# Down projection of an encoder layer: where the pieces of the second half's weights are kept, and in which order they are loaded

## The chip, the cores and the metric

The kernel runs on one core of a Trainium2 chip. The metric is the time of one execution on the device, in microseconds (us); lower is better. The profile names the engines PE (TensorE, matrix products; PEld is its weight load), DVE (VectorE), ACT (ScalarE), POOL (GpSimd) and SP (SyncE, which here only issues DMA transfers).

## The reference

One encoder layer over 1024 tokens of width 1024: a token mixer, a cross-attention and a gated feed-forward part, each followed by a layer norm. The change lies in the last product of the feed-forward part, `y @ w_down`, with `D_FF` = 2816 and `D` = 1024:

```python
def conv_ffn(x, w_up, b_up, w_dw, b_dw, w_down, b_down):
    h = x @ w_up + b_up
    h = lax.conv_general_dilated(h, w_dw[:, None, :], ...) + b_dw
    g, u = jnp.split(h, 2, axis=-1)
    y = jax.nn.gelu(g, approximate=False) * u
    return y @ w_down + b_down
...
    h = layer_norm(DN_ALPHA * h + conv_ffn(h, ...), ln3_w[l], ln3_b[l])
```

## The kernel before

**The product and its tiles.** The down projection contracts 22 slices of 128 features (`NFF` = 22, index `f`) for 8 tiles of 128 tokens (`NT` = 8, index `tt`) into 1024 columns, which are made in two halves of 512 (`c` = 0 and 1). Every operand is kept as a pair of 16-bit tiles, a high and a low part, and `mm3` makes each product with three matmuls of 128x512 (lines 225 to 227: high by high, high by low, low by high).

**Where y is kept.** `y` (22 slices) is written to DRAM by the stage before and comes back in pairs of slices: `y_pair(f, s)` loads a raw f32 tile named `ur` (a ring of two) and `split16` (lines 204 and 205) makes the pair: ACT writes the high part, DVE the low part. The pairs live in the tiles `yp` (list `yhome`, four slices to a tile); the sixth, `yhome[5]`, holds slices 20 and 21 in its first half and has two places free behind them. Slices 20 and 21 have a scale of their own, which a small matmul (`mx`) and five short DVE instructions work out shortly before (`y_scale(1)`, lines 184 to 177 and the one that writes `ratio`).

**Where the weights are kept.** `w_pair(j, c)` brings slices 4j to 4j+3 of half `c` (two slices for j = 5): one or two raw tiles `wraw` (a ring of two), each split by ACT and DVE into `whi` and `wlo`, which are rings of five. With six values of j and two halves the ring goes round more than twice, so a new piece waits until PE has done with the piece five places earlier. Only piece (5, 1), the last of half 1, has a place outside of the ring: the third slot of `yhome[5]`.

**The order of the work.** Half 0 is made first: for j = 0 to 4 a pass over the eight token tiles, which sum up in eight PSUM banks; a pass (the "NG loop", `NG` = 20) over slices 20 and 21 for the eight tiles follows, and DVE adds it to the copy `half0` with line 1773. Then the final loop takes one token tile after the other: 6 matmuls on slices 20 and 21 (bank `p2`), 60 matmuls on slices 0 to 19 (bank `p1`), the residual `r` (POOL lines 1792 and 1793, DVE line 1795), and the layer norm, whose result is written out. The residual rows of odd token tiles use the `wraw` ring too.

**What sets the order on each engine.** The program is written as above, with the calls of `w_pair` and `y_pair` between the token tiles, and a scheduler then places the instructions on each engine; every engine, and SP's DMA queue, works through its own list in order. Piece (5, 1) is the last `w_pair` of the program, and it is the first of half 1 that PE uses.

Of the kernel before, what the change touches and what calls it, by code (L numbers as in the profile page):

```python
# [8 lines left out]
F32 = mybir.dt.float32  # L9
# [47 lines left out]
def encoder(ctx, tc, I, out):  # L57
# [4 lines left out]
    def bcast_row(ap, n, off=0):  # L62
        return bass.AP(tensor=ap.tensor, offset=ap.offset + off, ap=[[0, 128], [1, n]])
# [15 lines left out]
    def bank(name):  # L79
        key = "mem" if name == "tk" else name  # L80
        turn[key] = turn.get(key, -1) + 1
        tag = SET[name][turn[key] % len(SET[name])]
        return pp.tile([128, 512], F32, name=name, tag=tag, bufs=NB[tag])
# [29 lines left out]
    def vec(i, name):  # L113
        t = vecs.tile([128, D], F32, name=f"vec{i}", tag=f"vec{i}")
        S.dma_start(t, bcast_row(I[name], D))
        return t
# [50 lines left out]
    def col(n=1):  # L167
        used[0] += n
        assert used[0] <= 96
        return sc[:, used[0] - n:used[0]]  # L170
# [32 lines left out]
    def split16(hi, lo, src, s):  # L203
        A.activation(hi, src, AF.Copy, scale=s)  # L204
        return V.scalar_tensor_tensor(lo, src, s, hi, op0=OP.mult, op1=OP.subtract)  # L205
# [76 lines left out]
    with ExitStack() as ca:  # L282

        yml = None
        with ExitStack() as cm:
# [254 lines left out]
            with ExitStack() as c2:  # L540
# [257 lines left out]
                with ExitStack() as c1:  # L798
# [7 lines left out]
                    for c in range(4):  # L806
                        w, ic = cw[2 + c]
                        for tt in range(NT):
# [6 lines left out]
                            j = slice(c % 2 * 256, c % 2 * 256 + 256)  # L815
# [407 lines left out]
    with ExitStack() as cb_:  # L1223
# [3 lines left out]
        f16 = lambda t: t.bitcast(F16)  # L1227
# [132 lines left out]
        def load_r(n):  # L1360
            if n < NT:
                rs[n] = rt.tile([128, D], F32, name="r", tag="r", bufs=5)
                S.dma_start(rs[n], h1_d[todo[n] * 128:todo[n] * 128 + 128, :])
# [74 lines left out]
        ur = cb_.enter_context(tc.tile_pool(name="unitraw", bufs=1, reuse_waits="tile"))  # L1438
# [126 lines left out]
        with ExitStack() as cE:  # L1565
# [69 lines left out]
            def y_pair(f, s):  # L1635

                raw = ur.tile([128, 2048], F32, name="ur", tag="ur", bufs=2)
                S.dma_start(raw.rearrange("p (f t) -> p f t", f=2), y_d[f:f + 2].rearrange("f p t -> p f t"))
                if f % 4 == 0:
                    tag = ("Yl", "X2h", "X1l", "X1h", "Yh", "X2l")[f // 4]  # L1640
                    pool = yp if tag[0] == "Y" else xp
                    yhome[f // 4] = f16(pool.tile([128, 4096], F32, name="yp", tag=tag)).rearrange(
                        "p (f n t) -> p f n t", f=4, n=2)
                for i in range(2):
                    t = yhome[f // 4][:, f % 4 + i]
                    split16(t[:, 0], t[:, 1], raw[:, i * SEQ:i * SEQ + SEQ], s)
                    ys[f + i] = t[:, 0], t[:, 1]

            def w_pair(j, c):

                n = min(4, NFF - 4 * j)
                if j == 5 and c == 1:
                    h, l = yhome[5][:, 2, 0], yhome[5][:, 2, 1]
                else:
                    h, l = (wp.tile([128, 2048], F16, name=t, tag=t, bufs=5) for t in ("whi", "wlo"))
                for i in range(n // 2):
                    raw = wp.tile([128, WP], F32, name="wraw", tag="wraw", bufs=2)[:, :1024]
                    S.dma_start(raw.rearrange("p (i c) -> p i c", i=2),
                                I["w_down"][2 * j + i].rearrange("p (i c) -> p i c", i=2)[:, :, c * 512:c * 512 + 512])
                    split16(h[:, i * 1024:i * 1024 + 1024], l[:, i * 1024:i * 1024 + 1024], raw, sd)  # L1660
                wdn[c, j] = tuple(t[:, :n * 512].rearrange("p (f c) -> p f c", c=512) for t in (h, l))

            def dmm(ps, tt, c, fs, first, last):
                t0 = slice(tt * 128, tt * 128 + 128)
                for f in fs:
                    wh, wl = wdn[c, f // 4]
                    mm3(ps, ys[f][0][:, t0], ys[f][1][:, t0], wh[:, f % 4, :], wl[:, f % 4, :],
                        first and f == fs[0], last and f == fs[-1])
# [3 lines left out]
            def y_scale(g):  # L1672
                sy[g] = scale_of(ysum[:, :NG] if g == 0 else ysum[:, NG:], 14)

            loaded = None
            for v in range(NFF):
# [25 lines left out]
                if v == NFF - 1:  # L1702
                    w_pair(0, 0)
# [20 lines left out]
            for tt in range(5):  # L1724
                ps[tt] = bank("dn")
                dmm(ps[tt], tt, 0, range(4), True, False)
                if tt == 0:
                    w_pair(1, 0)
                if tt in (1, 3):
                    y_pair(4 + tt - 1, s1)  # L1730
# [8 lines left out]
        with ExitStack() as cF:  # L1739
            wk = cF.enter_context(tc.tile_pool(name="wkF", bufs=1, reuse_waits="tile"))  # L1740
            inv = col(3)
            V.tensor_tensor(inv[:, 0:1], sd, s1, OP.mult)
            V.tensor_scalar(inv[:, 1:2], inv[:, 0:1], ALPHA, None, op0=OP.mult)
            V.tensor_scalar(inv[:, 2:3], inv[:, 0:1], inv[:, 0:1], EPS, op0=OP.mult, op1=OP.mult)
            al, ep = inv[:, 1:2], inv[:, 2:3]
            half0 = wk.tile([128, NT, 512], F32, name="half0")

            rw, rb, bd = vec(0, "ln2_w"), vec(1, "ln2_b"), vec(2, "b_down")
            V.tensor_scalar(rw, rw, al, None, op0=OP.mult)
            V.tensor_scalar(bd, bd, inv[:, 0:1], None, op0=OP.mult)  # L1750
            V.scalar_tensor_tensor(rb, rb, al, bd, op0=OP.mult, op1=OP.add)
            lw = vec(2, "ln3_w")
            for j in range(1, 5):
                for tt in range(NT):
                    dmm(ps[tt], tt, 0, range(4 * j, 4 * j + 4), False, j == 4)
                    if j == 4:
                        V.tensor_copy(half0[:, tt], ps[tt])
                    if tt in (0, 4) and j < 4:
                        y_pair(4 * j + 4 + tt // 2, s1)
                    if tt == 2:  # L1760
                        w_pair(j + 1, 0)
                    if j == 2 and tt == 6:
                        y_scale(1)
                        ratio = col()
                        V.tensor_scalar(ratio, sy[1][0], s1, 2.0 ** -14, op0=OP.mult, op1=OP.mult)
                    if j == 4 and tt == 0:
                        y_pair(NG, sy[1][1])
                    if j == 4 and tt in (4, 6):
                        w_pair((tt - 4) // 2, 1)
            for tt in range(NT):  # L1770
                p2 = bank("dn")
                dmm(p2, tt, 0, range(NG, NFF), True, True)
                V.scalar_tensor_tensor(half0[:, tt], p2, ratio, half0[:, tt], op0=OP.mult, op1=OP.add)
                if tt in (1, 3, 5):
                    w_pair(2 + tt // 2, 1)
            w_pair(5, 1)
            lb = yhome[5][:, 3].rearrange("p n t -> p (n t)").bitcast(F32)
            S.dma_start(lb, bcast_row(I["ln3_b"], D))
            rs = {}

            def load_r(tt):
                if tt < NT:
                    rs[tt] = (wp.tile([128, WP], F32, name="wraw", tag="wraw", bufs=2)[:, :D] if tt % 2 else
                              wk.tile([128, D], F32, name="r", tag="r", bufs=2))
                    S.dma_start(rs[tt], h2_d[tt * 128:(tt + 1) * 128, :])

            load_r(0)
            load_r(1)
            for tt in range(NT):
                load_r(tt + 2)  # L1790
                r = rs.pop(tt)
                G.tensor_tensor(r, r, rw, OP.mult)
                G.tensor_tensor(r, r, rb, OP.add)
                r0, r1 = r[:, :512], r[:, 512:]
                V.tensor_tensor(r0, r0, half0[:, tt], OP.add)
                p1, p2 = bank("dn"), bank("dn")
                dmm(p2, tt, 1, range(NG, NFF), True, True)
                V.scalar_tensor_tensor(r1, p2, ratio, r1, op0=OP.mult, op1=OP.add)
                dmm(p1, tt, 1, range(NG), True, True)
                V.tensor_tensor(r1, r1, p1, OP.add)  # L1800
                last = tt == NT - 1
                ln_tile(r, lw, lb, small, late=last, eps=ep, parts=2 if last else 1)
                for i in range(2 if last else 1):
                    c = slice(i * 512, i * 512 + 512) if last else slice(0, D)
                    (A if i else S).dma_start(out[tt * 128:(tt + 1) * 128, c], r[:, c])
# [87 lines left out]
```

## Time and profile before

| | us |
|---|---|
| median of 3 runs (lowest, highest) | 1573.36 (1570.8, 1579.4) |
| the profiled execution | 1571.99 |
| its span, first to last instruction | 1570.3 |

The profile is of one execution. The span is 1.7 us shorter than that execution's own time, which is what lies around it. The mean TensorE clock that was granted over the span is 0.976 of full speed (2.4 GHz).

### The profile page before, as it was taken

The page shows a single profiled execution, that of the slowest core. Times are in us where ns is not written, and L with a number is a line of the kernel's source. Part 1 is how long each engine was busy: PE and PEld are TensorE (multiplying, and loading weights), DVE is VectorE, ACT ScalarE, POOL GpSimd, SP SyncE. Part 2 cuts the span into 40 slices and gives each one's busy share as a digit, 9 for nine tenths or more (in the row PEclk, how much of TensorE's full clock was granted, in tenths as well). Part 3 has the DMA queues.
Part 4 walks back from the last instruction along what each step waited for, and adds up shares of the span by engine and source line. Part 5 has one row for each costly group of instructions (what it writes and reads, how often), then busy time and mean ns, then how long its engine had stood idle before and what let it go on. Part 6 is the DMA issues. An engine that isn't in the chain of part 4 may idle for free.

```text
span 1570.3 us, 21752 instructions
## 1 busy us (share of the span) xinstructions
PE 1476.7 (94%) x8134; PEld 881.3 (56%) x8134; DVE 1053.8 (67%) x1961; ACT 807.4 (51%) x1367; POOL 574.6 (37%) x446
## 2 busy tenths in 40 slices
PE   8798889999999899899999889999999999997998
PEld 6697767456766788774455434444444444443443
DVE  7984985445767777675457678788878878925333
ACT  5524544565554467523335668777777756611000
POOL 6423662412232766234112174444434420301342
PEclk9799999999999899999999989999999999998999
DMA  8743545323554743544001332222232434832111
GB/s 297 276 179 112 189 140 190 105 75 101 147 149 130 243 132 102 205 167 180 28 27 54 121 137 108 107 107 108 107 121 107 162 107 144 294 124 69 40 68 54
DMA packets 84896, 208.62 MB, mean 133 GB/s; under 512 B 7091, under 2 KB 36019, under 8 KB 81462
## 3 DMA queue, kind: packets, MB, share of 16 engines
q1 hardware_dynamic: 84496, 206.46, 37.9%
q8 instruction: 64, 1.05, 0.3%
q0 software_dynamic: 144, 0.49, 0.2%
q14 instruction: 42, 0.34, 0.1%
q10 hardware_dynamic: 150, 0.27, 0.0%
HBM read 158.34 MB, written 49.35 MB: 132 GB/s over the span
## 4 chain that ended last, share of the span: by engine, by line
PE 55%; DVE 20%; DMA 9%; ACT 9%; issue 4%; POOL 2%; SPq 1%; DVEq 0%; ACTq 0%; POOLq 0%
PE dn L227 5%; PE dn L226 5%; PE dn L225 5%; DMA sv<-in_w_down_dram 3%; PE S L225 3%; PE S L227 3%; PE S L226 3%; DVE wlo L205 3%; DVE cbuf L1586 2%; DVE cbuf L1587 2%; PE tk L225 2%; PE z L226 2%; PE z L227 2%; PE tk L226 2%; PE tk L227 2%
## 5 line engine op out<-in xcount | busy, mean ns | idle before, releaser
L225 PE MATMUL dn<-whi,yp 128*128 128x512 f16 x336 | 127.6, 383 | 1.4 <-ACT whi L204 1.4
L226 PE MATMUL dn<-wlo,yp 128*128 128x512 f16 x336 | 128.2, 382 | 0.0
L227 PE MATMUL dn<-whi,yp 128*128 128x512 f16 x336 | 128.2, 382 | 0.0
L1504 POOL TENSOR_TENSOR wraw<-ur 128x512 f32<-128x512 f32 x22 | 45.5, 2069 | 201.8 <-issue 187.3
L1586 DVE SCALAR_TENSOR_TENSOR cbuf<-C,wdw,cbuf 128x1024 f32<-128x1024 f32 x44 | 75.7, 1721 | 28.6 <-ACT cbuf L1585 28.5
L225 PEld LDWEIGHTS <-whi 128*128 128x128 f16 x540 | 53.6, 99 | 66.1 <-issue 7.7
L227 PEld LDWEIGHTS <-wlo 128*128 128x128 f16 x540 | 53.4, 99 | 59.8 <-DVE wlo L205 4.2
L226 PEld LDWEIGHTS <-whi 128*128 128x128 f16 x540 | 53.7, 99 | 54.6 <-issue 1.6
L205 DVE SCALAR_TENSOR_TENSOR wlo<-wraw,us,whi 128x1024 f16<-128x1024 f32 (+1 forms) x48 | 67.0, 1413 | 18.8 <-ACT whi L204 18.5
L253 ACT ACTIVATE r<-r,lnrs 128x1024 f32<-128x1024 f32 x19 | 23.6, 1243 | 101.7 <-DVE lnrs L252 101.7
L1587 DVE SCALAR_TENSOR_TENSOR cbuf<-C,wdw,cbuf 128x1024 f32<-128x1024 f32 x44 | 70.5, 1602 | 1.2
L204 ACT ACTIVATE whi<-wraw,us 128x1024 f16<-128x1024 f32 (+1 forms) x48 | 51.4, 1103 | 27.2 <-DVE us L177 22.3
L225 PEld LDWEIGHTS <-yp 128*128 128x128 f16 x352 | 34.6, 98 | 52.1 <-issue 11.5
L1585 ACT ACTIVATE cbuf<-C,bdw,wdw 128x1024 f32<-128x1024 f32 x44 | 54.5, 1238 | 10.5 <-DVE C L1622 9.7
L243 POOL TENSOR_TENSOR lnrs<-lnrs,mhalf 128x1 f32<-128x1 f32 x32 | 18.8, 589 | 110.7 <-DVE lnrs L242 93.1
L227 PEld LDWEIGHTS <-yp 128*128 128x128 f16 x352 | 34.6, 98 | 42.4 <-issue 1.4
L226 PEld LDWEIGHTS <-yp 128*128 128x128 f16 x352 | 34.7, 99 | 42.2 <-issue 1.4
L225 PE MATMUL tk<-whi,Bo 128*128 128x256 f16 (+1 forms) x192 | 53.6, 279 | 3.1 <-DVE stage L205 3.1
L226 PE MATMUL tk<-wlo,Be 128*128 128x256 f16 (+1 forms) x192 | 53.6, 279 | 2.1 <-DVE wlo L205 2.1
L225 PE MATMUL tk<-whi,Be 128*128 128x256 f16 (+1 forms) x192 | 53.9, 282 | 0.3 <-ACT whi L204 0.3
L227 PE MATMUL tk<-whi,Be 128*128 128x256 f16 (+1 forms) x192 | 53.6, 279 | 0.0
L226 PE MATMUL tk<-wlo,Bo 128*128 128x256 f16 (+1 forms) x192 | 53.2, 277 | 0.0
(496 smaller groups left out, 4855.4 us busy)
## 6 DMA issues: line engine op xcount, KB each, us to landing
ur<-in_w_up_dram SPq DMA_DIRECT2D x22, 1024.0 KB
sv<-in_w_down_dram SPq DMA_DIRECT2D x22, 512.0 KB
y<-cbuf SPq DMA_DIRECT2D x22, 512.0 KB
ur<-y SPq DMA_DIRECT2D x11, 1024.0 KB
wraw<-in_w_down_dram SPq DMA_DIRECT2D x22, 512.0 KB
r<-h SPq DMA_DIRECT2D x19, 512.0 KB
h<-r SPq DMA_DIRECT2D x16, 512.0 KB
wraw<-in_w_tok_dram SPq DMA_DIRECT2D x10, 512.0 KB
```

Source lines behind the costliest of these rows:

```text
L204: A.activation(hi, src, AF.Copy, scale=s)
L205: return V.scalar_tensor_tensor(lo, src, s, hi, op0=OP.mult, op1=OP.subtract)
L225: T.matmul(ps, lh, rh, start=first, stop=False, skip_group_check=skip)
L226: T.matmul(ps, lh, rl, start=False, stop=False, skip_group_check=skip)
L227: return T.matmul(ps, ll, rh, start=False, stop=last, skip_group_check=skip)
L243: G.tensor_tensor(rs[:, 0:1], rs[:, 0:1], mhalf[:, 0:1], OP.pow)
L253: A.activation(r, r, AF.Identity, scale=rs[:, 0:1], bias=rs[:, 1:2])
L1504: G.tensor_tensor(S1, A21, A22, OP.add)
L1585: A.activation(c, C[:, 1:SEQ + 1], AF.Identity, scale=wdw[:, 1, j:j + 1], bias=bdw[:, j:j + 1])
L1586: V.scalar_tensor_tensor(c, C[:, 0:SEQ], wdw[:, 0, j:j + 1], c, op0=OP.mult, op1=OP.add)
L1587: V.scalar_tensor_tensor(c, C[:, 2:SEQ + 2], wdw[:, 2, j:j + 1], c, op0=OP.mult, op1=OP.add)
```

## The change

Pieces (3, 1) and (4, 1) no longer go round the ring of five: each takes a tile of the `ur` ring, where the raw tiles of y were (one holds `h` in its first half and `l` in its second). Piece (5, 1) keeps its place but is now the first of half 1 to be loaded, even before (5, 0), and all the calls move up: token tiles 1, 3, 5, 7 of pass j = 4 call (5, 1), (0, 1), (1, 1), (2, 1), and token tiles 0 and 2 of the NG loop call (3, 1) and (4, 1).

```diff
@@ w_pair
                 if j == 5 and c == 1:
                     h, l = yhome[5][:, 2, 0], yhome[5][:, 2, 1]
+                elif j > 2 and c == 1:
+                    t = f16(ur.tile([128, 2048], F32, name="ur", tag="ur", bufs=2))
+                    h, l = t[:, :2048], t[:, 2048:]
                 else:
                     h, l = (wp.tile([128, 2048], F16, name=t, tag=t, bufs=5) for t in ("whi", "wlo"))
...
                     if j == 4 and tt == 0:
                         y_pair(NG, sy[1][1])
-                    if j == 4 and tt in (4, 6):
-                        w_pair((tt - 4) // 2, 1)
+                    if j == 4 and tt in (1, 3, 5, 7):
+                        w_pair((5, 0, 1, 2)[tt // 2], 1)
             for tt in range(NT):
                 p2 = bank("dn")
                 dmm(p2, tt, 0, range(NG, NFF), True, True)
                 V.scalar_tensor_tensor(half0[:, tt], p2, ratio, half0[:, tt], op0=OP.mult, op1=OP.add)
-                if tt in (1, 3, 5):
-                    w_pair(2 + tt // 2, 1)
-            w_pair(5, 1)
+                if tt in (0, 2):
+                    w_pair(3 + tt // 2, 1)
```

The instructions are the same in number on each engine; what moves is their order and the tiles that they name. Lines behind the first edit are three numbers higher after the change, those behind the last one two (1773 becomes 1776, 1795 becomes 1797).

ACT's list before the change, the splits of half 1's weights up to the final loop. The tiles `whi_12751`, `whi_12787`, `whi_12826`, `whi_12852`, `whi_12878` are pieces (0, 1) to (4, 1), and `yp_12688` is `yhome[5]`: its row with `ur_12686` is y's slices 20 and 21, its row with `wraw_12904` is piece (5, 1).

```order
L204 ACTIVATE whi_12751<-wraw_12753,sc_95 128x1024
L204 ACTIVATE whi_12751<-wraw_12757,sc_95 128x1024
L204 ACTIVATE whi_12787<-wraw_12789,sc_95 128x1024
L204 ACTIVATE whi_12787<-wraw_12793,sc_95 128x1024
L204 ACTIVATE whi_12826<-wraw_12828,sc_95 128x1024
L204 ACTIVATE whi_12826<-wraw_12832,sc_95 128x1024
L204 ACTIVATE yp_12688<-ur_12686,sc_95 128x1024 x2
L204 ACTIVATE whi_12852<-wraw_12854,sc_95 128x1024
L204 ACTIVATE whi_12852<-wraw_12858,sc_95 128x1024
L204 ACTIVATE whi_12878<-wraw_12880,sc_95 128x1024
L204 ACTIVATE whi_12878<-wraw_12884,sc_95 128x1024
L204 ACTIVATE yp_12688<-wraw_12904,sc_95 128x1024
```

ACT's list after the change, the same place; `whi_12723` is piece (5, 0), `whi_12742`, `whi_12778`, `whi_12814` are (0, 1) to (2, 1), `ur_12832` is (3, 1) and `ur_12857` (4, 1).

```order
L204 ACTIVATE yp_12688<-wraw_12706,sc_95 128x1024
L204 ACTIVATE whi_12723<-wraw_12725,sc_95 128x1024
L204 ACTIVATE whi_12742<-wraw_12744,sc_95 128x1024
L204 ACTIVATE whi_12742<-wraw_12748,sc_95 128x1024
L204 ACTIVATE whi_12778<-wraw_12780,sc_95 128x1024
L204 ACTIVATE whi_12778<-wraw_12784,sc_95 128x1024
L204 ACTIVATE whi_12814<-wraw_12816,sc_95 128x1024
L204 ACTIVATE whi_12814<-wraw_12820,sc_95 128x1024
L204 ACTIVATE ur_12832<-wraw_12833,sc_95 128x1024
L204 ACTIVATE ur_12832<-wraw_12837,sc_95 128x1024
L204 ACTIVATE yp_12688<-ur_12686,sc_95 128x1024 x2
L204 ACTIVATE ur_12857<-wraw_12858,sc_95 128x1024
```

Piece (5, 1) has moved from the last row to the first, ahead of (5, 0); y's slices 20 and 21 now stand behind both rows of (3, 1).

PE's list before the change, from the last matmul of the NG loop (`dn_12896`) into the final loop's first token tile (`dn_12919` is its bank `p2`, `dn_12918` its `p1`).

```order
L227 MATMUL dn_12896<-whi_12719,yp_12688 128x512
L225 LDWEIGHTS yp_12688
L225 MATMUL dn_12919<-yp_12688 128x512
L225 LDWEIGHTS yp_12043
L225 MATMUL dn_12918<-whi_12751,yp_12043 128x512
L226 LDWEIGHTS yp_12043
L226 MATMUL dn_12918<-wlo_12752,yp_12043 128x512
```

PE's list after the change, the same place (`dn_12917` is `p2`, `dn_12916` is `p1`).

```order
L227 MATMUL dn_12898<-whi_12723,yp_12688 128x512
L225 LDWEIGHTS yp_12688
L225 MATMUL dn_12917<-yp_12688 128x512
L226 LDWEIGHTS yp_12688
L226 MATMUL dn_12917<-yp_12688 128x512
L227 LDWEIGHTS yp_12688
L227 MATMUL dn_12917<-yp_12688 128x512
L225 LDWEIGHTS yp_12688
L225 MATMUL dn_12917<-yp_12688 128x512
L226 LDWEIGHTS yp_12688
L226 MATMUL dn_12917<-yp_12688 128x512
L227 LDWEIGHTS yp_12688
```

The first matmul behind the NG loop is the same in both, one that reads piece (5, 1); before, the other five of `p2` stood 21 matmuls further on, and now they follow at once.

DVE's list before the change, from the NG loop's third token tile to the residual of token tile 1 (`wraw_12911`; `r_12909` and `r_12913` are those of tiles 0 and 2).

```order
L1773 SCALAR_TENSOR_TENSOR half0_12296<-dn_12844,sc_95,half0_12296 128x512
L238 BN_STATS lnst_12988<-r_12909 128x6
L1795 TENSOR_TENSOR r_12913<-r_12913,half0_12296 128x512
L1773 SCALAR_TENSOR_TENSOR half0_12296<-dn_12862,sc_95,half0_12296 128x512
L1773 SCALAR_TENSOR_TENSOR half0_12296<-dn_12870,sc_95,half0_12296 128x512
L1773 SCALAR_TENSOR_TENSOR half0_12296<-dn_12888,sc_95,half0_12296 128x512
L1773 SCALAR_TENSOR_TENSOR half0_12296<-dn_12896,sc_95,half0_12296 128x512
L205 SCALAR_TENSOR_TENSOR wlo_12879<-wraw_12880,sc_95,whi_12878 128x1024
L205 SCALAR_TENSOR_TENSOR wlo_12879<-wraw_12884,sc_95,whi_12878 128x1024
L205 SCALAR_TENSOR_TENSOR yp_12688<-wraw_12904,sc_95,yp_12688 128x1024
L1795 TENSOR_TENSOR wraw_12911<-wraw_12911,half0_12296 128x512
```

DVE's list after the change, the same place (`wraw_12909` and `wraw_12999` are the residuals of token tiles 1 and 3).

```order
L1776 SCALAR_TENSOR_TENSOR half0_12296<-dn_12849,sc_95,half0_12296 128x512
L1797 TENSOR_TENSOR r_12911<-r_12911,half0_12296 128x512
L1776 SCALAR_TENSOR_TENSOR half0_12296<-dn_12866,sc_95,half0_12296 128x512
L1797 TENSOR_TENSOR wraw_12909<-wraw_12909,half0_12296 128x512
L1776 SCALAR_TENSOR_TENSOR half0_12296<-dn_12874,sc_95,half0_12296 128x512
L238 BN_STATS lnst_13074<-wraw_12909 128x6
L238 BN_STATS lnst_13162<-r_12911 128x6
L1776 SCALAR_TENSOR_TENSOR half0_12296<-dn_12882,sc_95,half0_12296 128x512
L1797 TENSOR_TENSOR wraw_12999<-wraw_12999,half0_12296 128x512
L1776 SCALAR_TENSOR_TENSOR half0_12296<-dn_12890,sc_95,half0_12296 128x512
L1776 SCALAR_TENSOR_TENSOR half0_12296<-dn_12898,sc_95,half0_12296 128x512
```

The weight splits are gone from this place, and the residuals of token tiles 1 and 3 have moved ahead of the last four of the eight rows that take the NG loop's banks.

## Rows read from the trace of the kernel before

**Rows 1.** The page: its first line.

```profile
span 1570.3 us, 21752 instructions
```

**Rows 2.** PE's waits, whole span: us in total, times, longest.

```profile
PE dn L225 <- ACT yp L204: 8.4, 1, 8.4
```

**Rows 3.** Stretches: from:to, us, each engine's busy us, PE's clock, DMA share, GB/s.

```profile
1343.60:1437.10 93.50, 93.48 (x435) 42.49 (x433) 55.25 (x52) 29.45 (x28) 13.22 (x4) 1.00 0.44 151
...
1437.10:1445.49 8.39, 0.00 (x0) 0.00 (x0) 3.25 (x4) 3.33 (x3) 0.00 (x0) 0.74 0.41 126
1445.49:1451.40 5.91, 5.91 (x14) 2.01 (x14) 1.26 (x1) 0.00 (x0) 5.55 (x3) 0.50 0.25 89
1451.40:1562.52 111.12, 111.11 (x515) 50.20 (x513) 38.78 (x63) 8.68 (x7) 44.60 (x24) 1.00 0.14 53
1562.52:1570.30 7.78, 0.00 (x0) 0.00 (x0) 4.45 (x8) 0.00 (x0) 0.92 (x1) 0.82 0.17 67
```

**Rows 4.** The chain that ended last, 1436 to 1446: start, us, what.

```profile
1436.87 0.23 PE dn L227
...
1437.17 1.16 ACT whi L204
...
1438.35 1.29 DVE wlo L205
...
1439.66 4.60 DMA wraw<-in_w_down_dram
...
1444.29 1.16 ACT yp L204
...
1445.49 0.59 PE dn L225
```

**Rows 5.** Timeline of ACT: the idle time before and its releaser in brackets.

```profile
1370.41 1.15 ACT L204 ACTIVATE whi<-wraw,sc 128x1024 f16<-128x1024 f32 x1 [2.92 <-DMA wraw<-in_w_down_dram]
...
1405.87 2.19 ACT L204 ACTIVATE whi<-wraw,sc 128x1024 f16<-128x1024 f32 x2 [18.17 <-PE dn L227]
1415.40 2.19 ACT L204 ACTIVATE yp<-ur,sc 128x1024 f16<-128x1024 f32 x2 [7.34 <-issue]
```

**Rows 6.** Timeline of SP's DMA issues.

```profile
1370.74 0.46 SPq L1778 DMA_DIRECT2D yp<-in_ln_b_dram  x1
...
1408.37 1.74 SPq L1658 DMA_DIRECT2D wraw<-in_w_down_dram  x2
...
1440.86 0.33 SPq L1785 DMA_DIRECT2D wraw<-h  x1
```

**Rows 7.** Timeline of DVE in pass j = 4 and at the NG loop's start.

```profile
1407.05 2.48 DVE L205 SCALAR_TENSOR_TENSOR wlo<-wraw,sc,whi 128x1024 f16<-128x1024 f32 x2 [18.04 <-ACT whi L204]
...
1414.46 0.29 DVE L184 TENSOR_REDUCE sc<-mx 128x1 f32<-128x128 f32 x1 [0.18 <-PE mx L183]
...
1415.23 0.20 DVE L1765 TENSOR_SCALAR sc<-sc 128x1 f32<-128x1 f32 x1
...
1417.01 2.47 DVE L205 SCALAR_TENSOR_TENSOR yp<-ur,sc,yp 128x1024 f16<-128x1024 f32 x2
...
1426.76 0.69 DVE L1757 COPY half<-dn 128x512 f32<-128x512 f32 x1 [1.90 <-PE dn L227]
```

**Rows 8.** Timeline of POOL, the residual of token tile 1.

```profile
1445.77 3.19 POOL L1792 TENSOR_TENSOR wraw<-wraw,vec 128x1024 f32<-128x1024 f32 x1 [74.08 <-DMA wraw<-h]
1449.04 2.34 POOL L1793 TENSOR_TENSOR wraw<-wraw,vec 128x1024 f32<-128x1024 f32 x1
```

**Rows 9.** Timeline of DVE, the same residual.

```profile
1451.41 2.81 DVE L1795 TENSOR_TENSOR wraw<-wraw,half 128x512 f32<-128x512 f32 x1 [4.66 <-POOL wraw L1793]
...
1455.46 0.73 DVE L1798 SCALAR_TENSOR_TENSOR r<-dn,sc,r 128x512 f32<-128x512 f32 x1
```

## The prediction

> **What bounds the kernel now.** I read the waits of PE first, since the page's first line gives a span of 1570.3 us [rows 1] and PE is busy for most of it. The longest wait of PE in the whole span is one of 8.4 us in the down projection [rows 2]: a matmul that reads a piece of weights waits for ACT, which writes that piece. The stretches show where it lies and what it costs [rows 3]. From 1343.60 to 1437.10 PE has no gap at clock 1.00; from 1437.10 to 1445.49 it does nothing; the 14 matmuls after that run at clock 0.50 (1.2 GHz of 2.4 GHz) and take 5.91 us; then it runs without a gap at clock 1.00 to 1562.52; the last 7.78 us are the layer norm of the last token tile. So ahead of the wait and behind it PE is the limit, and what PE loses in the middle is lost at the end.
>
> The chain of work names the wait's links [rows 4]. The NG loop's last matmul ends at 1437.10. It frees the place in the ring of five into which ACT then splits (4, 1): 1.16 us on ACT, 1.29 us on DVE. That frees a raw tile, and only now can the raw tile of (5, 1) be loaded: 4.60 us. ACT splits it in 1.16 us, and at 1445.49 PE has what its next matmul needs. The piece that is used first is at the end of a chain of four links that begins with PE itself.
>
> **The change part by part.** *The loading order.* (5, 1) takes the place in ACT's list where (5, 0) was, whose split ran at 1370.41 [rows 5]. Its own place was free by then: before the change SP issued the load of ln3_b into the same tile at 1370.74 [rows 6]. So (5, 1) is ready some 65 us before it is needed. (0, 1) and (1, 1) move back by one raw tile each, and still stand ahead of the split that waits for the end of pass j = 3. That split, of (2, 1), stays at 1405.87, since the ring gives it its place only then [rows 5], and its DVE part runs from 1407.05 for 2.48 us [rows 7].
>
> *The places of (3, 1) and (4, 1).* They no longer wait for PE. (3, 1) comes through the raw tiles that (2, 1) frees. SP issues two loads there, the first at 1408.37 [rows 6]; the second I put 1.2 us later, at 1409.6. I take 4.63 us from issue to ACT's start, from 1439.66 to 1444.29 [rows 4]. ACT splits at 1413.0 and 1414.2, and DVE is done with the second at about 1417.4, with one 0.69 us copy of a bank between. Behind it DVE makes the scale of y's slices 20 and 21, which lasted from 1414.46 to 1415.43 before [rows 7], and now ends near 1418.4. ACT then splits the two slices in 2.19 us [rows 5], DVE in 2.47 us [rows 7], done at about 1422.1 against 1419.5 before. The NG loop needs them at 1426.8, when the last pass ends (DVE copies its last bank at 1426.76) [rows 7]. So the moved work costs 2.6 us on ACT and DVE, hidden by 7.3 us of which 4.7 us are left. (4, 1) takes the raw tile of those slices once DVE has read it, at 1422.1, and is split by about 1426.6. PE comes to it 54 matmuls into the final loop, near 1448.7, so 22 us are to spare.
>
> *The final loop.* It has 8 x 66 = 528 matmuls. At 111.12 us for 515 [rows 3] one takes 0.2158 us. Its first matmul now has all it needs at 1437.10: the piece, y, and a bank that DVE frees while the NG loop runs. PE has no gap, so it has no cause to lose the clock, which stayed at 1.00 for 93.5 us of work without a gap just before [rows 3].
>
> *The sum.* The wait gives back 8.39 us. The 14 matmuls at half clock took 5.91 us and take 14 x 0.2158 = 3.02 us, which gives 2.89 us. The tail of 7.78 us and everything ahead of 1366 stay. 8.39 + 2.89 = 11.28, and the profiled execution's 1571.99 us becomes 1560.7 us. That execution is 1.4 us under the median of the runs shown, 1573.36; by the median it would be 1562.1. I forecast 1561. The bounds of the second term: 0 if the clock falls for another reason, 2.89 if it doesn't fall; I take the upper end, since the trace shows it low here only behind the gap.
>
> **The residuals that now come earlier.** The residual rows of token tiles 1 and 3 use the raw ring and were issued from 1440.86 on [rows 6]. Now the ring is free at about 1424.6 and 1426.6. POOL began 4.91 us after that issue [rows 6, 8], so now near 1429.5; with 3.19 us for the first and 2.34 us for each further one [rows 8], tile 1's second instruction, the third in POOL's new list, ends near 1437.4. In DVE's new list the row that adds tile 1's half stands ahead of the rows that free the NG loop's last four banks, so these wait until 1437.4 too. PE wants the first of these banks at token tile 2 of the final loop, 132 matmuls after 1437.10, at 1465.6. That is hidden with more than 20 us to spare.
>
> POOL's work also falls beside DVE's in the NG loop now. DVE's add of two SBUF tiles took 2.81 us beside POOL, and the add from a bank took 0.73 us beside it [rows 9]; the NG loop's first bank is complete 6 matmuls after 1426.8, at 1428.1, and even if DVE's first three rows from there (bank, residual, bank; some 0.73 us each) took four times as long, they would end at 1436.9, before the final loop begins.
>
> **The rivals.** *y's slices 20 and 21 come late.* They are the closest margin, 4.7 us: their scale on DVE and their split on ACT now stand behind both loads of (3, 1). If the second load took longer than 4.63 + 4.7 = 9.3 us, PE would wait at the NG loop's start. For it: three queues in a row, each in order. Against it: the loads at this place in the program have nothing beside them. A load that takes 12 us gives a wait of 2.7 us and up to 2.9 us of clock: 1563.4 to 1566.3. Slower than before needs a wait above 8.4 us, so a load of more than 17.7 us; with 26 us it would be 16.7 us of wait and 2.9 us of clock, 1580.3.
>
> *DVE's list holds up PE in the final loop.* If POOL or the residual's load were late, PE would wait at 1465.6 for a bank whose release stands behind the residual of tile 1. It takes a residual later than I work out by 24 us; then each further microsecond costs one. The Trainium skill, page "Perfetto Trace Analysis", section "Tensor Engine Instruction (MATMUL, LD_WEIGHTS)", says that ACT, DVE and GpSimd take their instructions strictly in order, so a bank's release can't pass the waiting add. By this rule the change has put a wait ahead of releases that had none, and with a residual 30 us late it would give 6 us and the clock's 2.9 us back, 1569.6; the trace's DVE does follow its list, and the measured load makes the add early enough.
>
> *The wait stays.* If (5, 1) in its tile, or the `ur` tiles, were held by something that I overlook, a wait of the same size would stand at 1437 or at the 54th matmul: 1572. Against it: the load of ln3_b went into that tile at 1370.74 [rows 6], and the raw tiles have no reader but the splits.
>
> *A short wait is left,* at some piece or bank, of 2 to 5 us without the clock's loss: 1563 to 1566.
>
> **How the numbers follow.** No gap at all: 0.80. y late by a little, or a short wait left: 0.10. The wait stays: 0.05. DVE's list: 0.02. y late by more than the old wait: 0.03. The likeliest gives 1561; by itself it lies between 1558 (the lowest run shown, 1570.8, less 11.3, and a microsecond and a half of spread) and 1564. The range goes up to 1567 to take in the small waits, which leaves about 0.1 above and some spread below. No change that can be told is within 0.5%, 7.9 us: faster means under 1565.5. The likeliest and most of the small waits are under it: 0.83. Within: the wait stays, the larger small waits, and the spread of the runs: 0.14. Slower: 0.03.
>
> **What the profile after would show.** Right: no wait of PE on ACT or DVE between 1343 and the end, clock 1.00 there, the final loop in 113.9 us from 1437, ACT's split of (5, 1) near 1370 and those of (3, 1) at 1413 and 1414, y's slices 20 and 21 done near 1422, the residual's add on DVE near 1437. Wrong: PE idle at 1426.8 (y), at 1437 (the piece or its bank), at 1448.7 ((4, 1)) or at 1465.6 (a bank); or a clock under 1.00 without a gap ahead of it.

## The result and the profile after

The changed kernel takes 1563.02 us (median of 7 runs, 1557.97 to 1567.73), the kernel before 1573.36 us (7 runs beside them, 1570.8 to 1579.4). The ratio is 0.9931, with a 95% interval of 0.9908 to 0.9953: 10.9 us less, between 7.4 and 14.5. The forecast was 1561 (1558 to 1567) and faster, by which it meant under 1565.5, half a per cent; the median is under it, and the interval reaches to just above 0.995. The profiled execution of the changed kernel has a span of 1561.3 us and took 1563.02 us.

PE's waits first, in the changed kernel, from 1310 to 1562: us in total, times, longest. Of the wait of [rows 2] nothing is left; the two that remain stand at the start of the down projection, and the kernel before has them too.

```profile
PE z L225 <- ACT C L1616: 2.4, 1, 2.4
PE dn L225 <- ACT whi L204: 1.4, 1, 1.4
```

The stretches of the changed kernel, with the columns of [rows 3]: the one before the final loop, the final loop from the start of its first matmul to the end of its last, and the tail.

```profile
1343.60:1437.10 93.50, 93.50 (x436) 42.60 (x435) 58.23 (x52) 33.89 (x32) 20.04 (x7) 1.00 0.51 176
...
1439.39:1553.52 114.13, 114.13 (x529) 51.57 (x527) 39.98 (x67) 8.69 (x7) 40.61 (x23) 1.00 0.14 51
1553.52:1561.30 7.78, 0.00 (x0) 0.00 (x0) 4.45 (x8) 0.00 (x0) 0.92 (x1) 0.68 0.17 67
```

PE is busy for all of the final loop at clock 1.00. Where [rows 3] add up to 125.42 us from the end of the NG loop to the end of the last matmul (8.39 + 5.91 + 111.12), it is 114.13 now from the start of the final loop's first matmul: 11.29 us less. The tail is the 7.78 us that it was.

These two stretches don't begin at quite the same point. A matmul's row lasts 0.38 us, but at full clock the next one starts 0.22 us after it, so the stretch before leaves out some of the wait. The rows of the kernel before for the NG loop's last matmul and the last of all, and the last of all in the changed kernel:

```profile
1436.71 0.38 PE L227 MATMUL dn<-whi,yp 128*128 128x512 f16 x1
...
1562.14 0.38 PE L227 MATMUL dn<-whi,yp 128*128 128x512 f16 x1
```

```profile
1553.14 0.38 PE L227 MATMUL dn<-ur,yp 128*128 128x512 f16 x1
```

From the start of the one to the start of the other it is 125.43 us before, and 113.96 now (from 1439.18, in the next rows): 11.47 us less. From here on I count in this way.

PE's timeline where the wait was: the NG loop's last matmul, and the final loop's first two behind it at the usual distance of 0.22 us.

```profile
1439.18 0.38 PE L227 MATMUL dn<-whi,yp 128*128 128x512 f16 x1
1439.39 0.38 PE L225 MATMUL dn<-yp 128*128 128x512 f16 x1
1439.61 0.38 PE L226 MATMUL dn<-yp 128*128 128x512 f16 x1
```

ACT's timeline of the changed kernel, the rows that answer to [rows 5]: the split of (5, 1), the first of (5, 0), then (2, 1), the two of (3, 1), y's slices 20 and 21, and (4, 1).

```profile
1371.54 1.15 ACT L204 ACTIVATE yp<-wraw,sc 128x1024 f16<-128x1024 f32 x1 [2.74 <-DMA wraw<-in_w_down_dram]
1375.18 1.15 ACT L204 ACTIVATE whi<-wraw,sc 128x1024 f16<-128x1024 f32 x1 [2.49 <-DMA wraw<-in_w_down_dram]
...
1408.29 2.19 ACT L204 ACTIVATE whi<-wraw,sc 128x1024 f16<-128x1024 f32 x2 [16.20 <-PE dn L227]
1415.11 1.15 ACT L204 ACTIVATE ur<-wraw,sc 128x1024 f16<-128x1024 f32 x1 [4.62 <-DMA wraw<-in_w_down_dram]
1417.12 1.15 ACT L204 ACTIVATE ur<-wraw,sc 128x1024 f16<-128x1024 f32 x1 [0.86 <-DMA wraw<-in_w_down_dram]
1420.38 2.19 ACT L204 ACTIVATE yp<-ur,sc 128x1024 f16<-128x1024 f32 x2 [2.12 <-DVE sc L177]
1424.08 2.19 ACT L204 ACTIVATE ur<-wraw,sc 128x1024 f16<-128x1024 f32 x2 [1.51 <-DVE yp L205]
```

Piece (5, 1) is split 68 us before PE reads it. Slices 20 and 21 now stand behind (3, 1), and their idle time ends with a scale (line 177 of DVE), as the prediction had it. This execution is 2.4 us late against that of before already at the split of (2, 1) (1408.29 against 1405.87), for a cause that the last section comes to.

DVE's timeline of the changed kernel from y's low parts on; then POOL's for the residual of token tile 1, which answers to [rows 8].

```profile
1421.57 2.48 DVE L205 SCALAR_TENSOR_TENSOR yp<-ur,sc,yp 128x1024 f16<-128x1024 f32 x2 [0.50 <-ACT yp L204]
...
1429.23 0.69 DVE L1760 COPY half<-dn 128x512 f32<-128x512 f32 x1 [0.29 <-PE dn L227]
...
1431.38 1.73 DVE L1797 TENSOR_TENSOR r<-r,half 128x512 f32<-128x512 f32 x1
...
1435.13 0.75 DVE L1797 TENSOR_TENSOR r<-r,half 128x512 f32<-128x512 f32 x1
1435.80 0.74 DVE L1776 SCALAR_TENSOR_TENSOR half<-dn,sc,half 128x512 f32<-128x512 f32 x1
1438.12 2.82 DVE L1797 TENSOR_TENSOR wraw<-wraw,half 128x512 f32<-128x512 f32 x1 [1.58 <-POOL wraw L1795]
1440.86 0.74 DVE L1776 SCALAR_TENSOR_TENSOR half<-dn,sc,half 128x512 f32<-128x512 f32 x1
...
1443.37 0.68 DVE L1797 TENSOR_TENSOR wraw<-wraw,half 128x512 f32<-128x512 f32 x1
1443.97 1.40 DVE L1776 SCALAR_TENSOR_TENSOR half<-dn,sc,half 128x512 f32<-128x512 f32 x2
...
1453.84 0.69 DVE L1802 TENSOR_TENSOR r<-r,dn 128x512 f32<-128x512 f32 x1 [7.82 <-PE dn L227]
```

```profile
1430.22 5.11 POOL L1794 TENSOR_TENSOR wraw<-wraw,vec 128x1024 f32<-128x1024 f32 x2 [57.34 <-DMA wraw<-h]
1435.29 5.10 POOL L1795 TENSOR_TENSOR wraw<-wraw,vec 128x1024 f32<-128x1024 f32 x2
```

The residual's add waits 1.58 us for POOL and runs for 2.82 us, and the last four banks of the NG loop (rows of line 1776 behind it) are free only at 1445.37. By 1453.84 DVE itself waits 7.82 us for PE: it has caught up, and PE never had to wait for a bank.

### The profile page after: what moved, and what is told of

Its sections match the earlier page's. It is cut to its first block, busy times and chain, and to the rows that moved or that the text cites. A ratio compares the mean times of both kernels' runs of the same rounds, so it can differ in the third digit from the quotient of the medians.

```text
span 1561.3 us, 21750 instructions
## 1 busy us (share of the span) xinstructions
PE 1475.0 (94%) x8134; PEld 879.5 (56%) x8134; DVE 1050.6 (67%) x1961; ACT 807.4 (52%) x1367; POOL 573.7 (37%) x446
## 4 chain that ended last, share of the span: by engine, by line
PE 54%; DVE 23%; ACT 9%; DMA 7%; issue 4%; POOL 2%; SPq 1%; DVEq 0%; ACTq 0%; POOLq 0%
PE dn L226 5%; PE dn L227 5%; PE dn L225 5%; PE S L225 3%; PE S L227 3%; PE S L226 3%; DVE wlo L205 3%; DMA sv<-in_w_down_dram 3%; DVE cbuf L1586 3%; DVE cbuf L1587 3%; PE cl L225 2%; PE cl L226 2%; PE cl L227 2%; PE tk L225 2%; PE tk L226 2%
## 5 line engine op out<-in xcount | busy, mean ns | idle before, releaser
L225 PE MATMUL dn<-whi,yp 128*128 128x512 f16 x272 | 102.1, 379 | 1.4 <-ACT whi L204 1.4
L226 PE MATMUL dn<-wlo,yp 128*128 128x512 f16 x272 | 103.2, 380 | 0.0
L227 PE MATMUL dn<-whi,yp 128*128 128x512 f16 x272 | 103.0, 379 | 0.0
L225 PE MATMUL tk<-whi,Bo 128*128 128x256 f16 (+1 forms) x192 | 54.6, 285 | 3.1 <-DVE stage L205 3.1
L225 PE MATMUL tk<-whi,Be 128*128 128x256 f16 (+1 forms) x192 | 54.0, 282 | 0.3 <-ACT whi L204 0.3
L227 PE MATMUL tk<-whi,Bo 128*128 128x256 f16 (+1 forms) x192 | 54.2, 282 | 0.0
```

Of the source, the lines that this page charges most:

```text
L225: T.matmul(ps, lh, rh, start=first, stop=False, skip_group_check=skip)
L226: T.matmul(ps, lh, rl, start=False, stop=False, skip_group_check=skip)
L227: return T.matmul(ps, ll, rh, start=False, stop=last, skip_group_check=skip)
```

## The experiments

My theory: the gain is one wait, with the clock's fall behind it, at the end of a chain of four links (PE frees a ring place, (4, 1) is split into it, its raw tile is loaded anew, (5, 1) is split). If so, cutting any one link takes away all of it, and the parts of the change do not add up. The rivals: the change's two parts are both needed, or give a gain of their own each; the clock's fall has another cause than the gap; the new order leaves so little room for y that the change stands at an edge.

**The changed kernel again** (`e0_after_again`), no edit, beside the three kernels that follow and on their chip.

> The changed kernel once more, on the chip on which its parts are run. Theory (the wait and the clock behind it are all that was gained): ratio to before 0.993, no wait of PE from the first pass of the down projection to the end, and 114 us from the end of the NG loop to the last matmul, against 125.4 us before. Rival (part of the measured gain is chance): 0.996 to 1.000.

Measured: 1565.01 us (7 runs) against 1575.73 (12 runs of the kernel before), ratio 0.9942, 0.9922 to 0.9963. PE's waits are the two above. The gain is there a second time, of the same size within its interval.

**The loading order alone** (`e1_order_alone`): the changed kernel with (3, 1) and (4, 1) in the ring of five, as before.

```diff
@@ w_pair (against the changed kernel)
-                elif j > 2 and c == 1:
-                    t = f16(ur.tile([128, 2048], F32, name="ur", tag="ur", bufs=2))
-                    h, l = t[:, :2048], t[:, 2048:]
```

> Only the order of loading is changed: (5, 1) first, but (3, 1) and (4, 1) in the ring of five as before. Theory (PE waited only because the piece used first came last): (5, 1) is ready near 1375; (4, 1) still waits for the NG loop's end, but is split within 4 us, and PE comes to it 11.6 us after that end, so there is no wait, ratio 0.993. Rival (the ring is what held PE up, and the places are needed): a wait of some us remains, at (4, 1), ratio 0.996 to 1.000.

Measured: 1562.57 us (6 runs), 0.9919 (0.9900 to 0.9938), no wait of PE at the final loop or in it. The split of (4, 1) still waits for the NG loop's last matmul, and that now costs nothing:

```profile
1440.16 2.19 ACT L204 ACTIVATE whi<-wraw,sc 128x1024 f16<-128x1024 f32 x2 [8.17 <-PE dn L227]
```

Both raw tiles are there by then, DVE has the low part by 1444.5, and PE comes to (4, 1) 54 matmuls after 1439.91, at 1451.6: 7 us to spare.

**The places alone** (`e2_places_alone`): the kernel before with the three lines of `w_pair`, in its own loading order.

```diff
@@ w_pair (against the kernel before)
+                elif j > 2 and c == 1:
+                    t = f16(ur.tile([128, 2048], F32, name="ur", tag="ur", bufs=2))
+                    h, l = t[:, :2048], t[:, 2048:]
```

> Only the places are changed: (3, 1) and (4, 1) in the raw tiles of y, and all pieces loaded in the old order with (5, 1) last. Theory: no piece waits for PE any more, so (5, 1), though last, is loaded from about 1427 and split by 1433, ahead of the NG loop's end: no wait, ratio 0.993, the same as the order alone. Rival (the order is what counts): (5, 1) is still late, a wait of 3 to 8 us remains, ratio 0.996 to 1.000.

Measured: 1562.0 us (6 runs), 0.9916 (0.9896 to 0.9936), no wait either. Piece (5, 1) is still the last that is loaded, but behind the split of (2, 1) no split waits for PE any more:

```profile
1422.66 2.19 ACT L204 ACTIVATE ur<-wraw,sc 128x1024 f16<-128x1024 f32 x2 [1.51 <-DVE yp L205]
1429.31 1.15 ACT L204 ACTIVATE yp<-wraw,sc 128x1024 f16<-128x1024 f32 x1 [4.46 <-DMA wraw<-in_w_down_dram]
```

DVE is done with it at 1431.8, and the final loop begins at 1437.85.

**PE's order of use alone** (`e6_pe_order_alone`): the kernel before, with loading and places as they were; in token tile 0 the 60 matmuls of `p1` come ahead of the 6 of `p2`.

```diff
@@ final loop (against the kernel before; dmm returns its last matmul)
                 p1, p2 = bank("dn"), bank("dn")
-                dmm(p2, tt, 1, range(NG, NFF), True, True)
+                if tt == 0:
+                    hold = dmm(p1, tt, 1, range(NG), True, True)
+                with (tc.issue_after(hold.ins) if tt == 0 else nullcontext()):
+                    dmm(p2, tt, 1, range(NG, NFF), True, True)
                 V.scalar_tensor_tensor(r1, p2, ratio, r1, op0=OP.mult, op1=OP.add)
-                dmm(p1, tt, 1, range(NG), True, True)
+                if tt > 0:
+                    dmm(p1, tt, 1, range(NG), True, True)
```

> Neither places nor loading order are changed; instead PE makes the 60 matmuls on slices 0 to 19 first in the final loop's first token tile, and the 6 that read (5, 1) after them. Theory (only the first use was early): (5, 1) comes 8.4 to 9.7 us after the NG loop's end and is used 12.9 us after it: no wait, ratio 0.993. Rival (loading is late for more than this piece, so that (4, 1) is missed now): a wait of some us at (4, 1) or (5, 1), ratio 0.996 to 1.000.

Measured: 1560.77 us (6 runs), 0.9913 (0.9892 to 0.9933), no wait. The chain runs as late as before, (4, 1) first and then (5, 1), beside 60 matmuls:

```profile
1440.89 2.19 ACT L204 ACTIVATE whi<-wraw,sc 128x1024 f16<-128x1024 f32 x2 [8.17 <-PE dn L227]
1447.66 1.15 ACT L204 ACTIVATE yp<-wraw,sc 128x1024 f16<-128x1024 f32 x1 [4.59 <-DMA wraw<-in_w_down_dram]
```

DVE is done at 1450.1 and PE's first matmul on (5, 1) starts at 1453.59: 3.5 us to spare.

**Two pieces swapped** (`e5_swap_two`): the kernel before with (5, 1) loaded just ahead of (4, 1), nothing else.

```diff
@@ NG loop (against the kernel before)
                 if tt in (1, 3, 5):
-                    w_pair(2 + tt // 2, 1)
-            w_pair(5, 1)
+                    w_pair((2, 3, 5)[tt // 2], 1)
+            w_pair(4, 1)
```

> The kernel before with one edit: (5, 1) is loaded ahead of (4, 1) instead of behind it. Theory: (5, 1) takes the raw tile that (3, 1) frees, near 1429, and is split by 1436, just ahead of the NG loop's end: no wait, or one below 1 us, and 114 to 115 us from the NG loop's end to the last matmul. Rival (one place earlier is not enough): a wait of 3 us or more.

Measured in one run: 1568.20 us, and 1568.56 for one of the kernel before. By the time alone the theory would have failed; the trace says otherwise. PE has no wait at the final loop, which begins at 1444.60, and ACT has the high part of (5, 1) 2.2 us ahead of that:

```profile
1441.24 1.15 ACT L204 ACTIVATE yp<-wraw,sc 128x1024 f16<-128x1024 f32 x1 [4.57 <-DMA wraw<-in_w_down_dram]
1445.64 1.15 ACT L204 ACTIVATE whi<-wraw,sc 128x1024 f16<-128x1024 f32 x1 [3.25 <-DMA wraw<-in_w_down_dram]
```

What is late is everything ahead: the down projection's first matmul starts at 1320.97, against 1314.44, 1313.86 and 1319.99 in the three single runs below, whose instructions up to there are the same (table below). So the trace shows that the wait and the slow matmuls are gone. That the lateness made up for them in the time is likely, but not shown, for the trace of the run of the kernel before beside it was not kept.

**The gap filled** (`e3_filled_wait`): the kernel before, with 36 more matmuls into `p1` at the gap, which `p1`'s own first matmul then overwrites. They depend on no late piece; PE's next matmul, on (5, 1), is tied behind them, and those of `p1` behind that one.

```diff
@@ final loop (against the kernel before; mm3 and dmm return their first matmul)
+                if tt == 0:
+                    for _ in range(36):
+                        fill = T.matmul(p1, ys[0][0][:, :128], wdn[1, 0][0][:, 0, :], start=True, stop=True)
+                    with tc.issue_after(fill.ins):
+                        m0 = dmm(p2, tt, 1, range(NG, NFF), True, True)
+                else:
+                    dmm(p2, tt, 1, range(NG, NFF), True, True)
                 V.scalar_tensor_tensor(r1, p2, ratio, r1, op0=OP.mult, op1=OP.add)
-                dmm(p1, tt, 1, range(NG), True, True)
+                with (tc.issue_after(m0.ins) if tt == 0 else nullcontext()):
+                    dmm(p1, tt, 1, range(NG), True, True)
```

> The kernel before, with 36 matmuls more that PE makes in the wait (into a bank that the next matmul starts afresh; nothing of the result is changed). They last 7.8 us of the wait's 8.4. Theory (2.9 us of the gain are the clock that fell in the wait): the wait's end stays 8.4 us after the NG loop's end, the clock stays at 1.00, and from the NG loop's end to the last matmul it is 122.5 us instead of 125.4. Rival (the clock falls for another reason, or the slow matmuls are no loss): 125.4.

Measured in one run: 1568.29 us, and 1568.56 for one of the kernel before; two single runs can't tell a difference of 3 us. PE's timeline (the fillers carry line 1802) and two stretches, the gap and the 5.85 us behind it:

```profile
1436.38 7.93 PE L1802 MATMUL dn<-whi,yp 128*128 128x512 f16 x36
1444.65 0.38 PE L225 MATMUL dn<-yp 128*128 128x512 f16 x1 [0.34 <-ACT yp L204]
```

```profile
1436.38:1444.65 8.27, 7.93 (x37) 3.53 (x36) 3.24 (x4) 3.33 (x3) 0.00 (x0) 1.00 0.40 129
1444.65:1450.50 5.85, 5.85 (x28) 2.66 (x28) 1.27 (x1) 0.00 (x0) 5.29 (x2) 1.00 0.30 90
```

The piece comes nearly as late as before, but the clock stays at 1.00, and 28 matmuls fit where the kernel before had 14 in 5.91 us [rows 3]. From the final loop's first matmul, on (5, 1), to the start of the last it is 113.74 us against 116.65 (1562.14 - 1445.49): 2.91 us less, for work that computes nothing. (The whole final loop in the table is 3.2 us shorter; the other 0.3 is that the piece came so much sooner here.) So the clock's term is a term of its own, and its cause is the gap.

**y later, once and twice** (`e4_y_later_1`, `e7_y_later_2`): the changed kernel, with the load and split of (3, 1) made two and three times over, called ahead of the NG loop, and the scale of slices 20 and 21 tied behind them by adding zero times a value of the low part. (4, 1) is called at token tile 2 as before.

```diff
@@ w_pair and the NG loop (against the changed kernel; y_pair loads, and returns its splits as a function; w_pair returns the low part)
-                for i in range(n // 2):
+                for i in list(range(n // 2)) * (2 if (j, c) == (3, 1) else 1):
...
-                        y_pair(NG, sy[1][1])
+                        late = y_pair(NG, sy[1][1], True)
...
+            l31, s2 = w_pair(3, 1), col()
+            V.scalar_tensor_tensor(s2, l31[:, 2047:], 0.0, sy[1][1], op0=OP.mult, op1=OP.add)
+            late(s2)
...
-                if tt in (0, 2):
-                    w_pair(3 + tt // 2, 1)
+                if tt == 2:
+                    w_pair(4, 1)
```

In the second kernel the 2 is a 3.

> The changed kernel, with the load and split of (3, 1) made twice and the split of y's slices 20 and 21 tied behind the second. It tries the margin that the prediction put at 4.7 us. Theory: the second copy adds about 7.1 us on DVE, of which some were idle before, so slice 20's high part is ready about a microsecond ahead of the NG loop and slice 21's low part just in time: a wait of 0 to 0.5 us. Rival (the margin is smaller): a wait of 2 us or more at the NG loop's start.

> As the run before, with the load and split of (3, 1) made three times. Theory: 7.1 us more, so PE waits about 6 us at the start of the NG loop, and the clock falls behind it, which costs up to 2.9 us more: 6 to 9 us lost. Rival (other work covers it): no wait.

Measured, one run each: 1559.36 and 1575.89 us, beside 1568.56 for one of the kernel before. In the first, ACT begins y's slices at 1423.73 and has slice 20 about 1.1 us later, at 1424.8; the NG loop's first matmul starts at 1425.44, so some 0.6 us are left, and PE waits for nothing:

```profile
1423.73 2.19 ACT L204 ACTIVATE yp<-ur,sc 128x1024 f16<-128x1024 f32 x2 [1.54 <-DVE sc L1779]
```

```profile
1425.44 0.38 PE L225 MATMUL dn<-whi,yp 128*128 128x512 f16 x1
1425.66 0.38 PE L226 MATMUL dn<-wlo,yp 128*128 128x512 f16 x1
1425.87 0.38 PE L225 MATMUL dn<-whi,yp 128*128 128x512 f16 x1
1426.09 0.38 PE L226 MATMUL dn<-wlo,yp 128*128 128x512 f16 x1
```

But PE's order differs there too. In the changed kernel the NG loop goes through lines 225, 226 and 227 in turn, and 227 reads y's low part, which DVE writes last; here, and in the second kernel, the scheduler put matmuls of line 227 further back. DVE has slice 21's low part only at 1427.39, and the changed kernel's order would want it by the sixth matmul, at 1426.52, so with that order I estimate a wait of 0.9 us. In the second PE waits at the NG loop, and the clock falls behind it:

```profile
1439.28 0.61 PE L225 MATMUL dn<-whi,yp 128*128 128x512 f16 x1 [5.85 <-ACT yp L204]
...
1444.37 0.51 PE L225 MATMUL dn<-whi,yp 128*128 128x512 f16 x1
1444.71 0.38 PE L226 MATMUL dn<-wlo,yp 128*128 128x512 f16 x1
```

```profile
1439.30:1445.20 5.90, 5.90 (x16) 2.16 (x17) 4.68 (x4) 3.15 (x3) 0.00 (x0) 0.55 0.25 86
```

The final loop behind it is as in the changed kernel. The price is 132.28 - 123.62 = 8.66 us up to there (table). The wait is 5.85 by its row and 6.01 from start to start; the 13 matmuls behind it take 5.43 us (1439.28 to 1444.71), where 13 x 0.2158 is 2.81, which makes 2.6 of clock. That rival is real: two more loads of 512 KB, with their splits, cost nothing or about 1 us, and four take most of the gain.

**All of them side by side.** From the traces, us: when the first matmul of the down projection starts, how long from there to the start of the final loop, and from there to the start of the last matmul. For the kernel before, the final loop is counted from where its first matmul would have started without the wait (1436.71 + 0.22), with the gap filled from the first filler.

| kernel | first matmul at | to the final loop | final loop | that execution |
|---|---|---|---|---|
| before | 1314.98 | 121.95 | 125.21 | 1571.99 |
| changed | 1315.77 | 123.62 | 113.75 | 1563.02 |
| changed, again | 1316.40 | 121.95 | 113.74 | 1561.94 |
| loading order alone | 1316.34 | 123.57 | 113.75 | 1563.52 |
| places alone | 1315.91 | 121.94 | 113.74 | 1561.47 |
| PE's order alone | 1317.01 | 123.63 | 113.74 | 1564.25 |
| two pieces swapped | 1320.97 | 123.63 | 113.74 | 1568.20 |
| gap filled | 1314.44 | 121.94 | 122.01 | 1568.29 |
| y later, once | 1313.86 | 121.94 | 113.75 | 1559.36 |
| y later, twice | 1319.99 | 132.28 | 113.74 | 1575.89 |

The final loop takes the same 113.74 or 113.75 us in every kernel whose gap is gone, whatever took it away, and each of the four cures alone has all of the 11.47 us. The ratios of three of them (0.9919, 0.9916, 0.9913) and that for both parts together on the same chip (0.9942) have intervals that overlap, and 11.47 us off 1575.73 would be 0.9927, which lies in each of them; the fourth, two pieces swapped, has one run and goes by its trace. So no version is shown to beat the changed kernel; the smallest edits do as well, with less room.

## Why the prediction was right

**The sum.** Predicted 8.39 us of wait and 2.89 us of clock, 11.28 in all; the final loop became 125.21 - 113.74 = 11.47 us shorter. The filled gap measures the second term by itself, 2.91 us. The first was 0.17 us too small: 8.39 is counted from the end of a matmul's row, and from where the next would have started it is 1445.49 - 1436.93 = 8.56. The loop as a whole was put at 113.9 us and takes 114.13 to the end of its last matmul, which adds what that matmul lasts beyond its distance of 0.2158 us.

**The whole execution.** The two profiled executions differ by 1571.99 - 1563.02 = 8.97 us, not 11.28. What did not hold is "everything ahead of 1366 stay[s]": the final loop begins 2.46 us later than it could have in that of before, 0.79 us of it ahead of the down projection and 1.67 us within it, and the table shows both to change from one execution to the next with the same instructions. The medians differ by 10.3 us and the ratio's interval holds 11.47, so this is the spread of single executions and no cost of the change. That the median came within 2.1 us of the forecast is partly luck: the seven runs spread over 10 us.

**The loads.** ACT's splits of (3, 1) were put at 1413.0 and 1414.2 and came at 1415.11 and 1417.12, or 1412.7 and 1414.7 with the 2.4 us by which all is late. The first load's term was right; the second came 0.5 us later than I took it. Slices 20 and 21 were put at 1422.1 and were done at 1424.05, 1421.6 on the same footing: ACT, idle for 2.12 us, began them as soon as the scale was there (1420.34, or 1417.9 on the same footing, where I took 1418.4). Their margin was put at 4.7 us and is 5.0, from there to the NG loop's first matmul at 1429.03. But that matmul does not read what is done last. It reads the high part of slice 20, which ACT has at about 1421.5; the low part of slice 21, done at 1424.05, is read by the sixth, at 1430.11. So the delay that PE would feel begins 6.1 us on; the last experiments show about where, harmless at one repetition (with PE's order changed) and a wait of 5.85 us at two.

**The residual of tile 1.** POOL's start was put at 1429.5 and the add on DVE after 1437.4; they came at 1430.22 and 1438.12 (1427.8 and 1435.7 on the same footing). POOL's four instructions took 2.55 us on average, between the two prices of [rows 8]. The bank that PE wants at token tile 2, at 1439.39 + 132 x 0.2158 = 1467.9, was free 22 us ahead of it. DVE's add took 2.82 us, of which 2.27 lie beside POOL's last instruction (which ends at 1440.39), and 0.68 us (the next one of the same shape, at 1443.37) when POOL was idle. The Trainium skill, page "GPSIMD Engine Reference", section "1. Specifications", lists that GpSimd's SBUF interfaces are shared with VectorE, with contention for VectorE's instructions with two SBUF inputs; this pair of rows agrees, and so does the row of line 1776 at 1435.80, which reads a bank and one SBUF tile and takes 0.74 us beside POOL. What such an add costs depends on when it begins: three of them began beside POOL, at 1431.38, 1435.13 and 1438.12, and took 1.73, 0.75 and 2.82 us, and each ended 0.55 us after the POOL instruction beside which it began (these ended at 1432.57, 1435.33 and 1440.39).

**The rival of DVE's list** had a mechanism that exists and a price of nothing. Four bank releases do stand behind the add that waits for POOL. The Trainium skill, page "Perfetto Trace Analysis", section "Tensor Engine Instruction (MATMUL, LD_WEIGHTS)", has VectorE take its instructions strictly in order; the trace agrees, for these rows start at 1440.86, as the add ends, though PE was done with the NG loop's last bank at 1439.6.

**What was not tried:** a kernel that takes both the loading order and PE's order, since the trace leaves no wait for it to remove.

## What to carry to other kernels

When PE waits for a piece of a ring, follow the chain of waits back until it comes to PE itself, and look which link is cheapest to cut: the piece's place in the loading order, its place in memory, or the order in which PE uses it. Each alone gave all that both did, so cost the wait once, and add the slow matmuls behind it (here 2.6 to 2.9 us, for a wait of 5.9 us as for one of 8.4). Where the effect is under one per cent, compare the stretch that the edit touches, not single executions: here the stretch repeats within 0.01 us, while what lies ahead of it moves by 7 us.

## What the runs showed of the hardware

**The clock's fall is not in proportion to the wait.** Behind 8.39 us of idle PE 14 matmuls ran at 1.2 GHz and cost 2.9 us [rows 3]; behind 5.85 us (y later, twice) 13 did and cost 2.6 us.

**Two short waits lose the clock in some executions and not in others.** At the start of the down projection every kernel here has a wait of 1.4 us, six matmuls, and one of 2.4 us. The 4.80 us behind the second, in the changed kernel and in the same kernel run again:

```profile
1319.60:1324.40 4.80, 4.75 (x15) 1.84 (x15) 4.72 (x5) 0.00 (x0) 0.00 (x0) 0.64 0.71 235
```

```profile
1320.28:1325.08 4.80, 4.80 (x23) 2.20 (x23) 4.68 (x5) 0.33 (x1) 0.00 (x0) 1.00 0.85 274
```

15 matmuls at a mean clock of 0.64 in the one, 23 at 1.00 in the other, of the same instructions behind the same waits. Five of the ten executions in the table show the first (the changed kernel, loading order alone, PE's order alone, two pieces swapped, y later twice), with 1.6 to 1.7 us more up to the final loop: 123.6 against 121.94. The Trainium skill, page "TensorE: Matmul & The Clock Gate", section "What's actually happening", says that the same kernel shows different numbers of slow matmuls at its start from run to run. Here, behind waits in the middle of a kernel, the traces show the like: eight or nine slow matmuls, or none. What decides it in a given execution, no run here tells.

**The part ahead moves by itself.** The first matmul of the down projection came between 1313.86 and 1320.97 over ten executions, with the same instructions in the same order on each engine up to there. Part of the 7 us is the clock again: from 215 to 230 us of the span the two latest executions (two pieces swapped; y later, twice) have a mean clock of 0.66 and 81 matmuls of PE, the kernel before 1.00 and 124. Where the rest arises I did not follow.
